# One hybrid encoder step on one core: a held-back last product, an output norm in place, and a later state product

## The chip, the cores and the metric

The kernel runs on one core of one Trainium2 chip. The metric is the device time of one execution in microseconds. The core has five engines that the text speaks of: TensorE (PE, matrix products; PEld is its weight load), VectorE (DVE), ScalarE (ACT), GpSimd (POOL) and SyncE (SP), which here issues every transfer.

## The reference

One layer of a streaming encoder is applied to two kinds of tokens that share all weights: 2048 prompt tokens with zero starting states, and 8 samples of 16 tokens with given states. All data are float32.

```
h = rms_norm(x);  p = h @ w_in
x = x + concat(GDN(p_gdn), RWKV7(p_rwkv)) @ w_out
up = rms_norm(x) @ w_up
gate = causal_dwconv(up[:, :2816])            # width 3, history from state
x = x + (silu(gate) * up[:, 2816:]) @ w_down  # w_down is 2816 x 1024
y = rms_norm(x) * norm_final
# GDN, per chunk:   S = g S + K^T V_new       # one state per sample and head
```

The outputs are y for both kinds of tokens and the new states, among them the gated delta state (GDN) of each sample: 8 samples, 4 heads, 128 x 128.

## The kernel before

Tokens lie along the free dimension, channels along the 128 partitions. The 2176 tokens are cut into five groups of 384, 512, 384, 384 and 512 columns; the fifth holds 384 prompt columns and the 128 sample columns. Each group has an input phase (norm, w_in, convolutions, results to DRAM) and an output phase (w_out, residual, norm, feed-forward network, final norm). The phases run in the order in0, in1, in2, out0, in3, out1, in4, out2, out3, out4. Beside them run two recurrences, GDN and RWKV, block by block of 128 tokens; their small products fill in between the large ones.

**Products.** A float32 product is made of three reduced-precision products: each operand is split into a high part (`whi`, `xh`, `ah`) and a low part (`wlo`, `xl`, `al`), and hi·hi, hi·lo and lo·hi are summed in PSUM (`mm3`). Weights arrive through SP in tiles `w` of up to 512 columns, ACT casts them to `whi` (L439), and DVE or POOL subtracts to get `wlo` (L443). There are four buffers each of `w`, `whi` and `wlo`, and four PSUM banks for the large products.

**The feed-forward part.** `up(i)` makes the gate product `psga` and the value product `psup` for one of 22 feature tiles. Then DVE multiplies `y` by `psup` (L1229), ACT casts the activation to `ah` (L1231), and POOL subtracts to get `al` (L1233). `down` multiplies a part of the activations (parts of 4, 4, 4, 4, 3 and 3 feature tiles) with w_down into eight output tiles `psd`, and DVE adds each to the residual `res[m]` (L1241). For all parts but the last, `down` is called after the first `up` of the next part, so that the newest activation has a whole `up` to become ready. The last part (feature tiles 19, 20, 21) follows its own `up(21)` directly.

**The end of a group.** During the last `down`, ACT squares each `res[m]` and DVE sums the squares into `acc`. The task `finish` starts 3000 ns of the planner's clock later: a product with ones (`psn`), two ACT activations that make the inverse root, then eight times a DVE multiply from `res[k]` into a tile `grs` (L1264) and a store to `y` (L1265, for the last group also L1267). `grs` has two buffers; `res` has eight.

**The order of the work.** A generator-driven planner (`drive`, `spawn`, `step`) writes PE's order by hand: it counts a clock of matmul time, and every `yield n` of a task says that its next products should stand at least n ns of that clock later. The order on the other engines and in SP's queue is set by the tile framework's scheduler, which simulates the program. Every engine executes its own queue in order.

**The sample's states.** In the fifth group's last GDN block, `gdn_block(..., samp=True)`, eight half-head updates are made: DVE masks `w` into `gwm` (L988), the task yields 1500 ns, SP loads the old state `gS`, POOL scales it, PE multiplies `pSs <- gwm, gkt` (128 x 512, plain float32), DVE subtracts it from the state (L995), and SP stores it. The tiles `gwm` and `gS` share the eight buffers of the tag `g2`.

The functions that the change touches and what calls them:

Of the kernel before, what the change touches and what calls it, by code (L numbers as in the profile page):

```python
# [17 lines left out]
MUL, ADD, SUB = ALU.mult, ALU.add, ALU.subtract  # L18
# [183 lines left out]
def bc(a, n):  # L202

    return a.unsqueeze(len(a.shape)).to_broadcast(list(a.shape) + [n])


class Build:
# [236 lines left out]
            out.append((hi, lo))  # L444
        return out

    def mm3(self, ps, w, xs):

        last = len(xs) - 1
        for k, (xh, xl) in enumerate(xs):  # L450
            hi, lo = w[k // 4]
            c = slice(128 * (k % 4), 128 * (k % 4) + 128)
            self.mm(ps, lhsT=hi[:, c], rhs=xh, start=k == 0, stop=False)
            self.mm(ps, lhsT=hi[:, c], rhs=xl, start=False, stop=False)
            self.mm(ps, lhsT=lo[:, c], rhs=xh, start=False, stop=k == last)
            if k % 2 or k == last:
                yield
# [401 lines left out]
    def gdn_block(self, g, i, samp=False):  # L859
        nc, rp = self.nc, self.rp  # L860
# [53 lines left out]
        for p in range(2):  # L914
            ps = self.psr("pKK").rearrange("p (h a t) -> p h a t", h=2, a=2)
# [9 lines left out]
        if samp:  # L925
# [10 lines left out]
            for h in range(4):  # L936
                ps = self.psr("pKS")[:, 0:256].rearrange("p (a t) -> p a t", a=2)
# [23 lines left out]
        w = self.g2("gw", False)  # L961
        nc.scalar.copy(w, pw)
        w = w.rearrange(H4, h=4)
# [19 lines left out]
        if samp:  # L983
            for h in range(4):
                for hf in range(2):
                    c = slice(4 * hf, 4 * hf + 4)
                    wm = self.g2("gwm")
                    nc.vector.tensor_tensor(wm, w[:, h, :].unsqueeze(1).to_broadcast([128, 4, 128]), bc(self.c(C_SEG, 8)[:, c], 128), MUL)  # L988
                    yield 1500
                    S0 = self.g2("gS0")  # L990
                    nc.sync.dma_start(S0, self.I["st_gdn"][h][:, c, :])
                    nc.gpsimd.tensor_tensor(S0, S0, bc(eg[:, h, 64 * hf + 15:64 * hf + 64:16], 128), MUL)
                    ps = self.psr("pSs")
                    self.mm(ps, lhsT=kt[:, h, :], rhs=wm.rearrange("p r t -> p (r t)"), start=True, stop=True)
                    nc.vector.tensor_tensor(S0, S0, ps.rearrange("p (r t) -> p r t", r=4), SUB)  # L995
                    nc.sync.dma_start(self.O["o_gdn_s"][h][:, c, :], S0)
        else:
            pS = self.psr("pS").rearrange(H4, h=4)
            for h in range(4):
                self.mm(pS[:, h, :], lhsT=kt[:, h, :], rhs=w[:, h, :], start=True, stop=True)  # L1000
            for h in range(4):
                nc.vector.scalar_tensor_tensor(SN[:, h, :], SN[:, h, :], eg[:, h, 127:128], pS[:, h, :], op0=MUL, op1=ADD)
# [179 lines left out]
    def phase_out(self, g):  # L1182
        nc, q = self.nc, self.q
        while g.done < 2 or any(t[2] is not None for t in g.tails):
            yield 500
        xs = []
        for k in range(KT):
            xs.append(self.x(g, F32))
            nc.sync.dma_start(xs[k], g.og[k])
        xs = [self.split_x(g, x) for x in xs]  # L1190
        yield LX
        res = []
        for m in range(8):
            w = self.split_w(self.I["w_out"][m])
            ps = self.psb(g, "pso")
            yield from self.mm3(ps, w, xs)
            res.append(self.t(g, "res", 8))
            self.load_tok(g, res[m], self.I["x"][m])
            nc.vector.tensor_tensor(res[m], res[m], ps, ADD)
            if m == 0:  # L1200
                rs = self.acc(g)
            self.sumsq(g, rs, res[m], m == 0)
        hs = [self.split_x(g, res[k], q("nf")[:, k:k + 1]) for k in range(KT)]
        norm = self.spawn(self.late_rms(g, rs, 3000))
        yield LX

        def gate(i, ps):
            y = self.t(g, "xin", NXI)
            self.conv(g, ps, rs, [self.fw[:, 3 * i + n:3 * i + n + 1] for n in range(3)], self.hf[:, i, :], self.sf[:, i], y)
            th = self.t(g, "gth")  # L1210
            nc.scalar.activation(th, y, AF.Tanh)
            nc.vector.scalar_tensor_tensor(y, th, 1.0, y, op0=ADD, op1=MUL)
            nc.gpsimd.tensor_tensor(y, y, rs, MUL)
            return y

        def up(i):
            pair, y = [], None
            for n, name in enumerate(("psga", "psup")):
                w = self.split_w(self.I["w_up"][2 * i + n])
                ps = self.psb(g, name)  # L1220
                yield from self.mm3(ps, w, hs)
                pair.append(ps)
                if n == 0 and norm[2] is None:
                    y = gate(i, ps)
            if y is None:
                yield from self.until(norm)
                y = gate(i, pair[0])
            ps = pair[1]
            nc.vector.tensor_tensor(y, y, ps, MUL)  # L1229
            hi = self.a(g, "ah", F32R)  # L1230
            nc.scalar.copy(hi, y)  # L1231
            lo = self.a(g, "al", F32R)
            nc.gpsimd.tensor_tensor(lo, y, hi.bitcast(F32), SUB)  # L1233
            return hi, lo

        def down(a, b, acts, acc=None):
            for m in range(8):
                w = self.split_w(self.I["w_down"][m][:, 128 * a:128 * b], b - a)
                ps = self.psb(g, "psd")
                yield from self.mm3(ps, w, acts)  # L1240
                nc.vector.tensor_tensor(res[m], res[m], ps, ADD)  # L1241
                if acc is not None:
                    self.sumsq(g, acc, res[m], m == 0)

        acts = {}
        for pi, (a, b) in enumerate(PARTS):
            for i in range(a, b):
                acts[i] = yield from up(i)
                if i == a and pi:
                    pa, pb_ = PARTS[pi - 1]  # L1250
                    yield from down(pa, pb_, [acts.pop(n) for n in range(pa, pb_)])
        pa, pb_ = PARTS[-1]
        acc = self.a(g, "acc")
        yield from down(pa, pb_, [acts.pop(n) for n in range(pa, pb_)], acc)
        self.spawn(self.finish(g, res, acc))

    def finish(self, g, res, rs):

        nc, q = self.nc, self.q
        yield 3000  # L1260
        self.rms(g, rs)
        for k in range(KT):
            y = self.t(g, "grs")
            nc.vector.scalar_tensor_tensor(y, res[k], q("no")[:, k:k + 1], rs, op0=MUL, op1=MUL)  # L1264
            nc.sync.dma_start(self.O["y"][k][:, g.t0:g.t0 + g.P], y[:, 0:g.P])  # L1265
            if g.S:
                nc.sync.dma_start(self.O["y"][k][:, self.tp:self.tp + 128], y[:, g.P:g.n])  # L1267
# [64 lines left out]
```

## Time and profile before

| | |
|---|---|
| median of 3 runs | 3533.35 us (3531.5 to 3534.01) |
| the profiled execution's own time | 3535.21 us |
| its span (first to last instruction) | 3533.4 us |
| PE busy | 3355.5 us (95%), 21661 matmuls |
| DVE / POOL / ACT busy | 2371.1 / 1843.7 / 1512.1 us |
| mean granted TensorE clock | 0.978 |

The kernel is bound by PE nearly everywhere, so its idle time and the stretches at a lower clock are what a change of order can win or lose. In the views below, a row of the timeline gives start and duration in us, engine, line, operation and tiles, and in brackets how long the engine sat idle before it and which instruction ended that. Rows of a line and operation that follow each other closely are merged, with their count.

### The profile page before, as it was taken

Reading aid. Unit: us, or ns where it says so; the run is one execution under the profiler, and the core shown is the slowest. Engines: PE = TensorE matmul, PEld = TensorE weight load, DVE = VectorE, ACT = ScalarE, POOL = GpSimd, SP = SyncE. Lnnn points to the kernel's source line nnn. Section 1 sums busy time; section 2 is a strip of 40 time slices with the busy share of each in tenths; the row PEclk is TensorE's granted clock in tenths of the full one; section 3 lists DMA queues with packets and bytes.
Section 4 is the critical chain, followed back from the end, with each engine's and each line's share of the span. In section 5 each row is a group of like instructions: output and inputs, shape, how many; then the busy total and the mean of one; then the engine's idle time right before and its main releaser. Section 6 shows DMA issues by size and latency. Waiting matters only on the chain. (4 is left out here: it accounts for less than half of the span.)

```text
span 3533.4 us, 60005 instructions
## 1 busy us (share of the span) xinstructions
PE 3355.5 (95%) x21661; PEld 2888.1 (82%) x21661; DVE 2371.1 (67%) x4277; ACT 1512.1 (43%) x2698; POOL 1843.7 (52%) x2335
## 2 busy tenths in 40 slices
PE   8979989999999989999999999899999999999997
PEld 7857778889999878778877667699988899988886
DVE  6777777787666776766565777676657665665444
ACT  5554444444333454443333545443333444453333
POOL 4546556556666545556444445466656355534442
PEclk9989999999999999999999999999999999999999
DMA  5544444453333444533233334533334533443332
GB/s 170 170 127 135 144 151 126 131 174 113 115 114 105 123 145 148 173 93 91 90 93 90 121 120 144 186 116 113 114 119 153 164 120 126 138 143 96 96 94 82
DMA packets 346265, 447.58 MB, mean 127 GB/s; under 512 B 30168, under 2 KB 194336, under 8 KB 345968
## 3 DMA queue, kind: packets, MB, share of 16 engines
q1 hardware_dynamic: 345968, 443.75, 40.5%
q8 instruction: 170, 2.79, 0.3%
q14 instruction: 127, 1.04, 0.1%
HBM read 372.60 MB, written 71.03 MB: 126 GB/s over the span
## 5 line engine op out<-in xcount | busy, mean ns | idle before, releaser
L439 ACT CAST whi<-w 128x512 fp32r<-128x512 f32 (+1 forms) x1070 | 651.4, 610 | 1101.9 <-PE psd L362 282.8
L443 POOL TENSOR_TENSOR wlo<-w,whi 128x512 fp32r<-128x512 f32 (+1 forms) x535 | 705.0, 1318 | 721.9 <-ACT whi L439 695.1
L362 PE MATMUL psi<-x,whi 128*128 128x384 f32 (+1 forms) x2480 | 730.9, 376 | 34.5 <-ACT x L515 16.1
L362 PEld LDWEIGHTS psi<-x,whi 128*128 128x128 f32 x2480 | 454.1, 194 | 96.1 <-issue 21.6
L362 PE MATMUL psga<-x,whi 128*128 128x384 f32 (+1 forms) x1760 | 502.4, 366 | 0.0
L362 PE MATMUL psup<-x,whi 128*128 128x384 f32 (+1 forms) x1760 | 497.1, 363 | 0.0
L443 DVE TENSOR_TENSOR wlo<-w,whi 128x512 fp32r<-128x512 f32 (+1 forms) x535 | 428.2, 800 | 79.5 <-ACT whi L439 78.9
L362 PE MATMUL psi<-x,wlo 128*128 128x384 f32 (+1 forms) x1240 | 453.7, 366 | 4.3 <-POOL wlo L443 4.1
L362 PEld LDWEIGHTS psga<-x,whi 128*128 128x128 f32 x1760 | 318.5, 190 | 28.8 <-issue 3.6
L362 PEld LDWEIGHTS psup<-x,whi 128*128 128x128 f32 x1760 | 315.6, 188 | 26.6 <-issue 1.8
L362 PE MATMUL psd<-ah,whi 128*128 128x384 f32 (+1 forms) x880 | 328.1, 373 | 5.8 <-ACT ah L1231 5.8
L362 PE MATMUL psd<-al,whi 128*128 128x384 f32 (+1 forms) x880 | 318.8, 362 | 5.0 <-POOL al L1233 5.0
L362 PE MATMUL psd<-ah,wlo 128*128 128x384 f32 (+1 forms) x880 | 318.5, 362 | 0.0
L362 PE MATMUL psga<-x,wlo 128*128 128x384 f32 (+1 forms) x880 | 316.3, 359 | 0.0
L362 PE MATMUL psup<-x,wlo 128*128 128x384 f32 (+1 forms) x880 | 314.5, 357 | 0.0
L1241 DVE TENSOR_TENSOR res<-res,psd 128x384 f32<-128x384 f32 (+1 forms) x240 | 145.3, 606 | 201.3 <-PE psd L362 200.2
L362 PEld LDWEIGHTS psi<-x,wlo 128*128 128x128 f32 x1240 | 240.0, 194 | 28.0 <-POOL wlo L443 7.1
L1233 POOL TENSOR_TENSOR al<-xin,ah 128x384 fp32r<-128x384 f32 (+1 forms) x110 | 125.9, 1145 | 143.8 <-ACT ah L1231 103.1
L839 DVE TENSOR_TENSOR TUr<-TUr,pX 128x256 f16<-128x256 f16 x396 | 149.1, 413 | 73.4 <-PE pX L362 72.1
L527 DVE TENSOR_TENSOR P<-psga,rsx 128x384 f32<-128x384 f32 (+1 forms) x110 | 64.3, 585 | 192.9 <-PE psga L362 186.9
L362 PE MATMUL pso<-x,whi 128*128 128x384 f32 (+1 forms) x640 | 185.5, 370 | 2.1 <-DVE x L513 0.9
L362 PEld LDWEIGHTS psd<-ah,whi 128*128 128x128 f32 x880 | 166.6, 189 | 22.0 <-ACT ah L1231 7.2
(342 smaller groups left out, 6759.6 us busy)
## 6 DMA issues: line engine op xcount, KB each, us to landing
w<-in_w_up SPq DMA_DIRECT2D x440, 256.0 KB, 2.7
w<-in_w_in SPq DMA_DIRECT2D x310, 256.0 KB, 2.7
w<-in_w_down SPq DMA_DIRECT2D x160, 256.0 KB, 2.7
rX<-rx SPq DMA_DIRECT2D x68, 320.0 KB, 4.4
w<-in_w_out SPq DMA_DIRECT2D x80, 256.0 KB, 3.0
w<-in_w_down SPq DMA_DIRECT2D x80, 192.0 KB, 2.4
rx<-res SPq DMA_DIRECT2D x48, 192.0 KB, 3.0
gd<-res SPq DMA_DIRECT2D x48, 192.0 KB, 2.8
```

Source lines behind the costliest of these rows:

```text
L362: self.nc.tensor.matmul(out, lhsT=lhsT, rhs=rhs, start=start, stop=stop)
L439: nc.scalar.copy(hi, w)
L443: eng.tensor_tensor(lo, w, hi.bitcast(F32), SUB)
L527: nc.vector.tensor_tensor(P[:, h:h + g.P], ps[:, 0:g.P], rs[:, 0:g.P], MUL)
L839: nc.vector.tensor_tensor(w, w, pX[:, y].rearrange("p u (n b) -> p u n b", b=b), ADD)
L1233: nc.gpsimd.tensor_tensor(lo, y, hi.bitcast(F32), SUB)
L1241: nc.vector.tensor_tensor(res[m], res[m], ps, ADD)
```

## The change

There are three edits and a helper argument.

1. `mm3` takes `part`, a range of feature tiles. `down` takes `lead`. For the last part of each group `lead` is 3: weights and PSUM banks of the first three output tiles are taken at once, the products of feature tiles 19 and 20 are made for all three, and only then those of feature tile 21, the newest. The additions to the residual and the sums of squares of these three follow together. The other five output tiles are done as before. This is done in all five groups.
2. `finish` writes the normalized result over `res[k]` in place of a `grs` tile.
3. The wait of the sample's GDN state task before each state product is 2500 ns of the planner's clock in place of 1500.

```diff
-    def mm3(self, ps, w, xs):
+    def mm3(self, ps, w, xs, part=None):
 
         last = len(xs) - 1
         for k, (xh, xl) in enumerate(xs):
+            if part and not part[0] <= k < part[1]:
+                continue
             hi, lo = w[k // 4]
...
-                    yield 1500
+                    yield 2500
                     S0 = self.g2("gS0")
...
-        def down(a, b, acts, acc=None):
-            for m in range(8):
-                w = self.split_w(self.I["w_down"][m][:, 128 * a:128 * b], b - a)
-                ps = self.psb(g, "psd")
-                yield from self.mm3(ps, w, acts)
+        def down(a, b, acts, acc=None, lead=0):
+            def add(m, ps):
                 nc.vector.tensor_tensor(res[m], res[m], ps, ADD)
                 if acc is not None:
                     self.sumsq(g, acc, res[m], m == 0)
+            weight = lambda m: self.split_w(self.I["w_down"][m][:, 128 * a:128 * b], b - a)
+            first = [(weight(m), self.psb(g, "psd")) for m in range(lead)]
+            for last in range(2):
+                for w, ps in first:
+                    yield from self.mm3(ps, w, acts, (b - a - 1, b - a) if last else (0, b - a - 1))
+            for m, (w, ps) in enumerate(first):
+                add(m, ps)
+            for m in range(lead, 8):
+                w = weight(m)
+                ps = self.psb(g, "psd")
+                yield from self.mm3(ps, w, acts)
+                add(m, ps)
...
-        yield from down(pa, pb_, [acts.pop(n) for n in range(pa, pb_)], acc)
+        yield from down(pa, pb_, [acts.pop(n) for n in range(pa, pb_)], acc, 3)
...
-            y = self.t(g, "grs")
-            nc.vector.scalar_tensor_tensor(y, res[k], q("no")[:, k:k + 1], rs, op0=MUL, op1=MUL)
+            y = res[k]
+            nc.vector.scalar_tensor_tensor(y, y, q("no")[:, k:k + 1], rs, op0=MUL, op1=MUL)
```

Three places in the program's order follow. The first is PE at the start of the last `down` of the fifth group; the number behind a tile's name tells one tile from another, and the newest activation is `ah_39340` before and `ah_39308` now. Before, the whole first output tile:

```order
L362 MATMUL psd_39351<-ah_39008,whi_39347 128x512
L362 MATMUL psd_39351<-al_39010,whi_39347 128x512
L362 MATMUL psd_39351<-ah_39008,wlo_39349 128x512
L362 MATMUL psd_39351<-ah_39242,whi_39347 128x512
L362 MATMUL psd_39351<-al_39244,whi_39347 128x512
L362 MATMUL psd_39351<-ah_39242,wlo_39349 128x512
L362 MATMUL psd_39351<-ah_39340,whi_39347 128x512
L362 MATMUL psd_39351<-al_39342,whi_39347 128x512
L362 MATMUL psd_39351<-ah_39340,wlo_39349 128x512
```

Now, the end of the third tile's two older activations, and then the newest for the first and second tile:

```order
L362 MATMUL psd_39333<-ah_39210,whi_39329 128x512
L362 MATMUL psd_39333<-al_39212,whi_39329 128x512
L362 MATMUL psd_39333<-ah_39210,wlo_39331 128x512
L362 MATMUL psd_39319<-ah_39308,whi_39315 128x512
L362 MATMUL psd_39319<-al_39310,whi_39315 128x512
L362 MATMUL psd_39319<-ah_39308,wlo_39317 128x512
L362 MATMUL psd_39326<-ah_39308,whi_39322 128x512
L362 MATMUL psd_39326<-al_39310,whi_39322 128x512
```

The first use of the newest activation stood behind 6 products of this `down`, and now stands behind 18. In the first group four small products `pR` of a recurrence stand behind the first 12 of them.

The second place is DVE after the second group's last `down`, where the input phase of the fifth group begins (`rsx` is its sum of squares, `x` its split input). Before:

```order
L1264 SCALAR_TENSOR_TENSOR grs<-res,par,acc 128x512 x2
L484 TENSOR_TENSOR rsx<-rsx,xin 128x512
L443 TENSOR_TENSOR wlo<-w_23786,whi 128x512
L484 TENSOR_TENSOR rsx<-rsx,xin 128x512
L1101 TENSOR_REDUCE rs<-pY 128x4
L1264 SCALAR_TENSOR_TENSOR grs<-res,par,acc 128x512
L1138 TENSOR_TENSOR SR<-SRc,pSr 128x128
L1104 TENSOR_TENSOR ryc<-pY,rs 128x256
L1264 SCALAR_TENSOR_TENSOR grs<-res,par,acc 128x512
```

Now:

```order
L486 TENSOR_TENSOR rsx<-rsx,xin 128x512
L1275 SCALAR_TENSOR_TENSOR res<-res,par,acc 128x512 x8
L486 TENSOR_TENSOR rsx<-rsx,xin 128x512
L443 TENSOR_TENSOR wlo<-w_23770,whi 128x512
L1103 TENSOR_REDUCE rs<-pY 128x4
L1140 TENSOR_TENSOR SR<-SRc,pSr 128x128
L486 TENSOR_TENSOR rsx<-rsx,xin 128x512
```

The eight multiplies stood in groups of one or two among other work, and now stand in one run of eight, ahead of the last two additions to `rsx`. A run of eight stands so after each of the first four groups; after the fifth nothing else is left on DVE.

The third place is PE at the sample's first state product. Before:

```order
L362 MATMUL po<-con,gKS 128x128
L362 MATMUL po<-gw,gAQ 128x128
L362 MATMUL pSs<-gwm,gkt 128x512
L362 MATMUL psga<-x,whi 128x384 x2
L362 MATMUL psga<-x,wlo 128x384
L362 MATMUL psga<-x,whi 128x384 x2
```

Now, from the end of the gate product:

```order
L362 MATMUL psga<-x,whi 128x384 x2
L362 MATMUL psga<-x,wlo 128x384
L362 MATMUL pA<-rX 128x256 x4
L372 MATMUL pT_31016<-con,rX 128x128 x3
L362 MATMUL pSs<-gwm,gkt 128x512
L372 MATMUL ptr<-con,ryc 128x128 x2
```

Between the last `po` and the first `pSs` stood nothing; now stand all 24 products of a `psga` and the recurrence's `pA` and `pT`. Ahead of the third state product stand four `pZ` before, and `pZ`, 12 large products and four `pR` now; ahead of the fourth, 6 large products and four `pR` before, and 12 and four `pR` now.

## Prediction

> **What bounds the kernel now.** I read the page first, then the waits of PE, then the timeline of PE with its feeders at the three places that the change touches, and the granted clock there.
>
> ```profile
> span 3533.4 us, 60005 instructions
> PE 3355.5 (95%) x21661; PEld 2888.1 (82%) x21661; DVE 2371.1 (67%) x4277; ACT 1512.1 (43%) x2698; POOL 1843.7 (52%) x2335
> PE pSs L362 <- DVE gwm L988: 7.3, 4, 4.9
> PE psd L362 <- ACT ah L1231: 5.8, 4, 2.0
> PE psd L362 <- POOL al L1233: 5.0, 5, 1.4
> ```
>
> PE is busy for 95% of the span, so 178 us in all are idle. The three waits (us in total, times, longest) are 18.1 us of them: PE waits for the newest activation's high part `ah`, for its low part `al`, and for the masked tile `gwm`. They lie here:
>
> ```profile
> 1212.63 0.34 PE L362 MATMUL psd<-ah,whi 128*128 128x384 f32 x1
> 1213.52 0.34 PE L362 MATMUL psd<-ah,wlo 128*128 128x384 f32 x1
> 1215.79 0.44 PE L362 MATMUL psd<-ah,whi 128*128 128x384 f32 x1 [1.93 <-ACT ah L1231]
> 1217.63 0.69 PE L362 MATMUL psd<-al,whi 128*128 128x384 f32 x1 [1.40 <-POOL al L1233]
> 1983.59 0.39 PE L362 MATMUL psd<-ah,whi 128*128 128x512 f32 x1
> 1986.17 0.49 PE L362 MATMUL psd<-ah,whi 128*128 128x512 f32 x1 [0.90 <-ACT ah L1231]
> 1987.54 0.50 PE L362 MATMUL psd<-al,whi 128*128 128x512 f32 x1 [0.87 <-POOL al L1233]
> 2732.36 0.44 PE L362 MATMUL psd<-al,whi 128*128 128x384 f32 x1 [0.80 <-POOL al L1233]
> 3085.35 0.33 PE L362 MATMUL psd<-ah,whi 128*128 128x384 f32 x1
> 3088.54 0.44 PE L362 MATMUL psd<-ah,whi 128*128 128x384 f32 x1 [2.00 <-ACT ah L1231]
> 3090.08 0.44 PE L362 MATMUL psd<-al,whi 128*128 128x384 f32 x1 [1.09 <-POOL al L1233]
> 3494.25 0.40 PE L362 MATMUL psd<-ah,whi 128*128 128x512 f32 x1
> 3495.41 0.39 PE L362 MATMUL psd<-ah,wlo 128*128 128x512 f32 x1
> 3496.78 0.51 PE L362 MATMUL psd<-ah,whi 128*128 128x512 f32 x1 [0.98 <-ACT ah L1231]
> 3498.13 0.50 PE L362 MATMUL psd<-al,whi 128*128 128x512 f32 x1 [0.84 <-POOL al L1233]
> ```
>
> In each of the five groups PE starts the last `down`, makes the six products of the older activations, and stands still. Six starts span 0.89 us in the first group (five steps of 0.178 us, 384 columns) and 1.16 us in the fifth (0.232 us, 512 columns). The clock after such waits is the eighth number of these windows (span, busy times and counts, PEclk, DMA share, GB/s):
>
> ```profile
> 1217.60:1220.40 2.80, 2.77 (x9) 2.47 (x10) 0.94 (x2) 1.04 (x2) 1.00 (x1) 0.50 0.13 50
> 1988.50:1991.50 3.00, 3.00 (x9) 1.99 (x7) 2.28 (x4) 1.50 (x4) 1.56 (x1) 0.52 0.06 12
> 2732.40:2736.00 3.60, 3.60 (x33) 3.35 (x33) 3.60 (x8) 1.87 (x4) 2.44 (x3) 1.00 0.23 64
> 3091.00:3094.50 3.50, 3.50 (x13) 3.50 (x12) 3.50 (x7) 2.66 (x6) 1.01 (x1) 0.52 0.29 92
> 2646.80:2650.60 3.80, 3.79 (x9) 2.77 (x10) 1.15 (x2) 0.00 (x0) 0.00 (x0) 0.50 0.13 45
> ```
>
> After the waits of the first, second and fourth group the clock is halved for 2.8, 3.0 and 3.5 us, and for 3.8 us after the state wait; after that of the third it stays full. Half of each slow stretch is lost: 1.4, 1.4, 1.7 and 1.9 us.
>
> **Edit 1, the newest product last.** No work is added. `ah` and `al` hang on the `up` ahead, whose rows don't move, so they come when they came; PE now asks for them 18 products after the start. The low part came when the products `psd<-al` above started.
>
> - First group: 18 products, four `pR` (0.28 us by the row at 1250.60 below) and one product of `ah` end at 1212.63 + 19 x 0.178 + 0.28 = 1216.29; `al` is there at 1217.63. 1.34 us of 3.33 stay: gain 2.0.
> - Second: 18 x 0.232 from 1983.59 is 1987.8, `al` is there at 1987.54. All 1.77 go.
> - Third: only 0.80 us is there, and it goes.
> - Fourth: 19 x 0.178 from 3085.35 is 3088.73, `al` is there at 3090.08: 1.35 us of 3.09 stay, gain 1.7.
> - Fifth: 3494.25 + 18 x 0.232 = 3498.43, `al` is there at 3498.13: 1.8 go.
>
> That is 8.1 us. Of the slow stretches I count the second group's 1.4 us as gone, since no wait is left there, and the other two as staying. Edit 1 gains 9.5 us. Its bounds: nothing, if the next products then wait as much longer, and 12.6 with the other two stretches (3.1) gone. Three of four weight buffers are held until the newest products are done; the fifth tile's weights come free behind 21 products and are wanted behind 36, which are 15 x 0.178 = 2.7 us for a cast (0.61) and a POOL subtraction (1.32), by these rows:
>
> ```profile
> L439 ACT CAST whi<-w 128x512 fp32r<-128x512 f32 (+1 forms) x1070 | 651.4, 610 | 1101.9 <-PE psd L362 282.8
> L443 POOL TENSOR_TENSOR wlo<-w,whi 128x512 fp32r<-128x512 f32 (+1 forms) x535 | 705.0, 1318 | 721.9 <-ACT whi L439 695.1
> ```
>
> **Edit 2, the last norm in place.** At the end of the program DVE waits for the stores that empty `grs`:
>
> ```profile
> 3519.52 1.42 DVE L1264 SCALAR_TENSOR_TENSOR grs<-res,par,acc 128x512 f32<-128x512 f32 x2 [3.88 <-ACT acc L502]
> 3522.53 0.75 DVE L1264 SCALAR_TENSOR_TENSOR grs<-res,par,acc 128x512 f32<-128x512 f32 x1 [1.60 <-DMA out_y<-grs]
> 3520.30 0.34 SPq L1265 DMA_DIRECT2D out_y<-grs  x1
> 3521.22 0.38 SPq L1265 DMA_DIRECT2D out_y<-grs  x1
> 3530.65 0.43 SPq L1267 DMA_DIRECT2D out_y<-grs  x1
> DMA packets 2304, 2.10 MB, mean 110 GB/s; under 512 B 256, under 2 KB 2304, under 8 KB 2304
> ```
>
> Without that wait the eight multiplies take 8 x 0.71 = 5.7 us, and SP's pace decides: two stores per tile every 0.92 us (3520.30 to 3521.22). The last store then starts near 3520.30 + 7 x 0.92 + 0.39 = 3527.1, not at 3530.65: gain 3.5 us. The 2.10 MB would flow in some 7 us, 300 GB/s; if they flow slower, down to 250 GB/s, 8.4 us are needed and 2 us are gained. I take 3.5.
>
> After the first four groups the run of eight meets other work. What goes and what comes there:
>
> ```profile
> 1250.60 0.28 PE L362 MATMUL pR<-TUr,Nhr 128*128 128x64 f16 x4 [1.71 <-DVE TUr L839]
> 1249.60 0.62 DVE L1264 SCALAR_TENSOR_TENSOR grs<-res,par,acc 128x384 f32<-128x384 f32 x1 [2.32 <-DMA out_y<-grs]
> 2029.27 0.97 PE L362 MATMUL pA<-rX 64*128 64x256 f32 x4 [2.26 <-ACT rtok L1050]
> 2020.24 1.02 PE L362 MATMUL psn<-rsx,con 128*128 128x512 f32 x2
> ```
>
> In the first group PE waited 1.71 us behind a DVE queue that stood 2.32 us for a store; that goes, and the 2.26 us in the second may. In the second, six more multiplies (6 x 0.7 = 4.2 us) stand ahead of the last additions to `rsx`, for which PE's `psn` at 2020.24 is queued, with all input products behind it: up to 4.2 us come. 1.71 + 2.26 against 4.2 is nothing: I take 0, with bounds of 4 us gained and 6 us lost (4.2 and a slow stretch of 1.9).
>
> **Edit 3, the state product later.**
>
> ```profile
> 2641.54 0.39 PE L362 MATMUL po<-gw,gAQ 128*128 128x128 f32 x2
> 2646.81 2.05 PE L362 MATMUL pSs<-gwm,gkt 128*128 128x512 f32 x2 [4.88 <-DVE gwm L988]
> 2652.89 1.13 PE L362 MATMUL pA<-rX 64*128 64x256 f32 x8
> ```
>
> Between `po` and the first `pSs` now stand 24 products of 384 columns (24 x 0.178 = 4.3 us) and `pA` with its transposes (some 1.1 us by the row at 2652.89). `po` ended near 2641.8, so `pSs` is reached near 2641.8 + 5.4 = 2647.2, after 2646.81: the 4.88 us go, and with them the slow stretch of 1.9. Gain 6.8 us. The three later waits (7.3 - 4.9 = 2.4 us) I leave in, since `gwm` also waits for buffers; with them it is 9.2. The lower bound is 2, if the gate product's weights or a PSUM bank come late in the place to which it is moved up.
>
> **The sum.** 9.5 + 3.5 + 0 + 6.8 = 19.8 us from the span of 3533.4. The profiled execution took 3535.21, 1.8 more than its span, and the median of the runs, 3533.35, stands at the span. So 3533.35 - 19.8 = 3513.6, rounded 3514.
>
> A rule weighed: the Trainium skill (TensorE: Matmul & The Clock Gate, section What's actually happening) says that the clock is halved after an idle window of about 3.4 us, comes back after a busy one, and that the windows run free. The slow stretches here (2.8 to 3.8 us) agree in length; but the second group's waits, 1.77 us together, were followed by one, which the rule does not give. By that rule the 1.3 us that stay in the first and fourth group halve nothing, and the sum would be 22.9 us, 3510.5; that is inside the second case below.
>
> **The rivals.**
> - *All of it goes* (3508): the two slow stretches (3.1) and the three later state waits (2.4) go too. For it: single waits of 0.80 us (third group) left the clock at 1.00, and the state products now stand wider. Against: 1.3 us are more than 0.80.
> - *The waits pass on* (3523): PE comes earlier to the next products and waits there, since DVE and ACT are no faster; the 9.5 us of edit 1 are lost. For it: after the first group PE already waits for DVE (the 1.71 us above), which edit 1 makes no faster; against: the fifth group has nothing behind it but its norm.
>
> - *The change does not do what it says* (3530): the newest product and `gwm` come late again, each behind what was moved ahead of it, and only the end of the program gains 3.5. Against it stand the margins of 0.2 to 0.4 us (second and fifth group, state), worked out above; they are small.
> - *Slower* (3542): the run of eight holds DVE at each of the first four ends, and PE waits it out in full: 3 x 8 x 0.62 + 5.7 = 20.6 us, and four slow stretches of 1.9 (7.6 us), against 19.8 gained. It decides from 5 us a boundary on. For it: `psn` and `wlo` stand behind the run. Against: only the second group's `psn` follows closely enough.
>
> **How the numbers follow.** Chances: forecast 0.43, all goes 0.24, passes on 0.20, not as said 0.07, slower 0.06. What a measurement of this kernel can tell from no change is about 0.2%, 7 us: 3526.3 to 3540.4. Forecast, all goes and the greater part of passes on lie below: faster 0.85; same 0.10, slower 0.05. The range goes from 3504 (the second case, with the 4 us that edit 2 may gain in the middle) to 3526 (the third case with 3 us of edit 2's losses).
>
> **What would show it.** In the changed profile PE's waits for `ah` and `al` should be near 3 us in total, not 10.8, and lie in the first and fourth group; the wait for `gwm` should be under 3 us; no clock of 0.5 at the second group's end and after `po`; the last eight multiplies without a wait for a store, and some 10.5 us from the first of them to the end, not 13.9. A new wait of `psn` for `rsx` after the second group's end of about 4 us would show the price of the run. The prediction is wrong if PE's waits elsewhere, in the first 20 us behind a group's end above all, grow by over 5 us.

## The result and the profile after

The changed kernel took 3515.5 us (median of four executions, 3511.93 to 3515.74) beside 3533.68 of the kernel before: a ratio of 0.9946, 95% interval 0.9935 to 0.9958. The forecast was 3514 in a range of 3504 to 3526. In the experiments the whole change was timed again, five executions beside 17 of the kernel before: a ratio of 0.9958 (0.9944 to 0.9971), which is 14.8 us. So the time came out as forecast, the gain is 15 to 19 us rather than 19.8, and it is not made up as the sum had it.

Of the changed kernel, the span, PE's row, and its waits (us in total, times, longest):

```profile
span 3513.7 us, 59988 instructions
PE 3343.0 (95%) x21661; PEld 2877.8 (82%) x21661; DVE 2377.6 (68%) x4277; ACT 1509.5 (43%) x2698; POOL 1844.4 (52%) x2335
PE pX L362 <- DVE Rr L823: 14.3, 13, 3.4
PE psn L362 <- DVE rsx L486: 8.4, 5, 4.0
PE psn L362 <- DVE acc L486: 8.2, 5, 3.7
PE psd L362 <- POOL al L1235: 2.3, 2, 1.2
PE pSs L362 <- DVE gwm L990: 2.0, 2, 1.3
```

The same waits of the kernel before, those that the prediction didn't show, and two more that the experiments come to (for `rtok` of a recurrence, and for `P` of the input phase):

```profile
PE pX L362 <- DVE Rr L821: 8.1, 9, 2.5
PE pA L362 <- ACT rtok L1050: 6.0, 3, 2.3
PE psg L372 <- DVE P L527: 5.0, 3, 1.8
PE psn L362 <- DVE rsx L484: 4.4, 4, 1.5
PE psn L362 <- DVE acc L484: 3.2, 3, 2.2
```

The waits that the change aims at fell: `psd` from 10.8 to 2.3 us, `pSs` from 7.3 to 2.0. Three others grew by 6.2, 4.0 and 5.0 us. PE's idle time, span less busy time, went from 3533.4 - 3355.5 = 177.9 us to 3513.7 - 3343.0 = 170.7: 7.2 us of 19.7. The other 12.5 us are busy time: the same 21661 matmuls took less, at a mean granted clock of 0.981 in place of 0.978.

Where the two profiles part, read at PE's products with ones (`psn`), which stand once at each norm. Before (the row of the second `rsx` stands in the prediction):

```profile
1234.35 0.91 PE L362 MATMUL psn<-acc,con 128*128 128x384 f32 x2 [0.33 <-DVE acc L484]
1247.03 0.81 PE L362 MATMUL psn<-rsx,con 128*128 128x384 f32 x2
2009.17 1.13 PE L362 MATMUL psn<-acc,con 128*128 128x512 f32 x2
2752.59 0.91 PE L362 MATMUL psn<-acc,con 128*128 128x384 f32 x2 [0.63 <-DVE acc L484]
3105.86 0.81 PE L362 MATMUL psn<-acc,con 128*128 128x384 f32 x2
3515.69 1.13 PE L362 MATMUL psn<-acc,con 128*128 128x512 f32 x2 [2.23 <-DVE acc L484]
```

After:

```profile
1229.75 0.91 PE L362 MATMUL psn<-acc,con 128*128 128x384 f32 x2 [1.24 <-DVE acc L486]
1246.42 0.81 PE L362 MATMUL psn<-rsx,con 128*128 128x384 f32 x2
2001.24 1.12 PE L362 MATMUL psn<-acc,con 128*128 128x512 f32 x2 [0.56 <-DVE acc L486]
2016.14 1.12 PE L362 MATMUL psn<-rsx,con 128*128 128x512 f32 x2 [4.01 <-DVE rsx L486]
2738.47 0.91 PE L362 MATMUL psn<-acc,con 128*128 128x384 f32 x2 [0.43 <-DVE acc L486]
3089.36 1.65 PE L362 MATMUL psn<-acc,con 128*128 128x384 f32 x2 [3.73 <-DVE acc L486]
3498.40 1.92 PE L362 MATMUL psn<-acc,con 128*128 128x512 f32 x2 [2.23 <-DVE acc L486]
```

The lead is 4.6 us at the first group's `acc`, 0.6 at the `rsx` behind it, 7.9 and 4.1 at the second group's pair, 14.1 and 16.5 at the third's and fourth's `acc`, 17.3 at the fifth's, and 19.7 at the end. After the first and the second group 4 us are given back each time. Both times a run of eight multiplies stands in DVE's queue:

```profile
1235.22 5.33 DVE L1275 SCALAR_TENSOR_TENSOR res<-res,par,acc 128x384 f32<-128x384 f32 x8 [0.75 <-ACT acc L504]
2008.36 5.39 DVE L1275 SCALAR_TENSOR_TENSOR res<-res,par,acc 128x512 f32<-128x512 f32 x8 [0.85 <-ACT acc L504]
3503.01 5.39 DVE L1275 SCALAR_TENSOR_TENSOR res<-res,par,acc 128x512 f32<-128x512 f32 x8 [4.67 <-ACT acc L504]
```

In the first group a recurrence's `Rr` is queued behind the run, and PE waits 3.38 us for it; in the second the last additions to `rsx` are, and PE waits 4.01 us. In the third row, at the end of the program, nothing waits: the eight go through, and 3513.7 - 3503.01 = 10.7 us are left from the first of them to the end, where 13.9 were before.

```profile
1241.41 0.28 PE L362 MATMUL pX<-Rr,TUr 128*128 128x64 f16 x4 [3.38 <-DVE Rr L823]
1215.52 0.45 PE L362 MATMUL psd<-al,whi 128*128 128x384 f32 x1 [1.24 <-POOL al L1235]
3073.28 0.45 PE L362 MATMUL psd<-al,whi 128*128 128x384 f32 x1 [1.08 <-POOL al L1235]
```

The last two rows are all that is left of the wait for the newest activation, in the first and fourth group. The windows (the eighth number is the granted clock) behind the first of these waits, behind the 3.38 us, and behind the fourth group's `psn`:

```profile
1217.50:1221.50 4.00, 4.00 (x27) 3.84 (x27) 4.00 (x10) 3.01 (x7) 1.56 (x3) 1.00 0.60 194
1242.00:1245.50 3.50, 3.50 (x14) 3.50 (x13) 1.78 (x4) 0.62 (x1) 0.39 (x1) 0.56 0.74 235
3089.00:3092.50 3.50, 3.14 (x7) 2.19 (x8) 0.30 (x1) 1.44 (x2) 0.00 (x0) 0.51 0.29 105
```

The short wait left the clock whole; the new long ones halved it.

In the third group the wait of 0.80 us for the newest activation is gone too, but PE, which comes earlier, waits longer for a transfer there, the one that brings a recurrence's state `rS`. Before:

```profile
2739.45 1.12 PE L362 MATMUL pZT<-rX,rS 64*64 64x32 f32 x32 [1.01 <-DMA rS<-in_st_rwkv]
```

After, with the window behind it, at half the clock for 6.8 us:

```profile
2722.39 1.12 PE L362 MATMUL pZT<-rX,rS 64*64 64x32 f32 x32 [1.92 <-DMA rS<-in_st_rwkv]
2723.80:2730.60 6.80, 6.80 (x30) 6.80 (x29) 2.28 (x5) 2.14 (x5) 1.48 (x3) 0.50 0.83 255
```

This repeats: the longest such wait in the third group is 0.54 to 1.04 us in all six profiles without edit 1, and 1.71 to 1.92 in all seven with its three tiles, of the two kernels and of the runs below.

### The profile page after: what moved, and what is told of

Its sections match the earlier page's. It is cut to its first block, busy times and chain, and to the rows that moved or that the text cites. A ratio compares the mean times of both kernels' runs of the same rounds, so it can differ in the third digit from the quotient of the medians.

```text
span 3513.7 us, 59988 instructions
## 1 busy us (share of the span) xinstructions
PE 3343.0 (95%) x21661; PEld 2877.8 (82%) x21661; DVE 2377.6 (68%) x4277; ACT 1509.5 (43%) x2698; POOL 1844.4 (52%) x2335
## 3 DMA queue, kind: packets, MB, share of 16 engines
q14 instruction: 127, 1.04, 0.1%
## 5 line engine op out<-in xcount | busy, mean ns | idle before, releaser
L362 PE MATMUL psi<-x,whi 128*128 128x384 f32 (+1 forms) x2480 | 727.0, 374 | 31.2 <-ACT x L517 14.1
L362 PEld LDWEIGHTS psd<-al,whi 128*128 128x128 f32 x880 | 166.3, 189 | 16.6 <-POOL al L1235 2.9
```

What stands on the lines that cost most here:

```text
L362: self.nc.tensor.matmul(out, lhsT=lhsT, rhs=rhs, start=start, stop=stop)
```

## The experiments

My theory after the two traces: edits 1 and 3 remove what they aim at; part of edit 1's gain passes on, because PE now reaches `psn` before DVE has the sum of squares; edit 2 gains at the end and costs, behind the run of eight, about what the waits for stores cost before. The rivals: the single edits are worth their terms in the sum (9.5, 3.5, 6.8); in place costs several us in the middle; or the profiles' differences are chance, since the slow stretches fall differently in every execution. That last one sets the precision: 29 executions of the kernel before, in the first study, lie between 3521.39 and 3539.62 us, with a standard deviation of 4.1. So each verdict below goes by several executions, 5 to 12 of each kernel. The runs come from three studies, each with executions of the kernel before of its own (29, 17 and 17); kernels of different studies are compared by their ratios. "Later sum" in the table means that `finish` of the first four groups waits 6000 ns in place of 3000. Gains in us are the ratio's distance from 1 times 3530, the mean time of the kernel before over the 46 executions of the first two studies (3530.1).

| kernel | ratio to the kernel before | 95% interval | gain, us |
|---|---|---|---|
| edit 1 alone | 0.9990 | 0.9980 to 0.9999 | 3.5 |
| edit 2 alone | 0.9988 | 0.9978 to 0.9998 | 4.2 |
| edit 3 alone | 0.9983 | 0.9974 to 0.9992 | 6.0 |
| whole change | 0.9958 | 0.9944 to 0.9971 | 14.8 |
| all edits, in place in the last group only | 0.9967 | 0.9955 to 0.9979 | 11.6 |
| in place in the last group, nothing else | 0.9985 | 0.9976 to 0.9994 | 5.3 |
| later sum, nothing else | 0.9993 | 0.9984 to 1.0001 | 2.5 |
| edit 1 and later sum | 0.9952 | 0.9939 to 0.9965 | 16.9 |
| whole change and later sum | 0.9932 | 0.9918 to 0.9946 | 24.0 |
| the same, in place in the last group only | 0.9928 | 0.9913 to 0.9943 | 25.4 |
| whole change and later sum, without edit 1 | 0.9959 | 0.9948 to 0.9971 | 14.5 |
| whole change and later sum, `lead` of 4 | 0.9941 | 0.9929 to 0.9953 | 20.8 |

### The edits alone

Edit 1 alone is the change of `mm3` and `down`, with `grs` and 1500 kept:

```diff
-        yield from down(pa, pb_, [acts.pop(n) for n in range(pa, pb_)], acc)
+        yield from down(pa, pb_, [acts.pop(n) for n in range(pa, pb_)], acc, 3)
```

> Edit 1 alone: the newest activation's products come last over three output tiles; the output norm has its own tiles and the state task waits 1500 ns as before. The forecast's terms: 9.5 us off the kernel before (8.1 idle, 1.4 slow clock). The rival that the waits pass on: under 3 us, because PE meets DVE earlier (the changed kernel's wait of 3.73 us for the sum of squares in the fourth group and those for the norm). If the chance placing of slow-clock stretches (1.7 us each in the profiles) dominates, anything from 4 to 15 us, and the runs of this one kernel would differ among themselves by steps of 1.7 us.

It gave 3.5 us. Three of PE's waits in it:

```profile
PE psg L372 <- DVE P L529: 9.1, 3, 4.7
PE psn L362 <- DVE acc L486: 8.1, 5, 3.8
PE pA L362 <- ACT rtok L1052: 8.1, 3, 4.5
```

The 8.5 us at `psd` are gone, as in the whole change (2.3 are left), but `psn<-acc` grew by 4.9 us (3.2 before), `psg<-P` by 4.1 and `pA<-rtok` by 2.1. The longest of the last two (4.7 and 4.5 us) stand after the first and the second group, behind the multiplies into the two `grs` tiles; the next section shows rows of such waits. PE's idle time in this execution is 3525.9 - 3348.6 = 177.3 us, where it was 177.9: the waits passed on in full, and nearly all that its span is shorter by is busy time (6.9 of 7.5 us).

Why PE waits at `psn`, seen in the fourth group. These windows go from the first product of the last `down` to `psn`, before and with edit 1 (span, then the busy times of PE, PEld and DVE):

```profile
3085.35:3105.86 20.51, 17.42 (x86) 16.37 (x86) 17.76 (x30) 13.71 (x26) 7.14 (x7) 0.92 0.54 174
3076.91:3097.75 20.84, 16.00 (x85) 14.55 (x84) 20.12 (x30) 14.89 (x28) 9.24 (x8) 0.98 0.54 183
```

The stretch did not get shorter: what edit 1 takes away at `psd`, PE now waits at `psn`. DVE has the same 30 instructions to do in both, and is now idle for only 0.72 us, so it sets the pace. Its instructions also take 2.4 us longer. Nearly all of that are the seven additions to `acc` (6.91 us against 4.72): three of them took some 1.6 us, each while POOL made a `wlo`, where those that run beside no POOL instruction took 0.55. The product `psn` stands 12 products behind the end of `down` in both. The first three output tiles are now all finished within the last nine of 27 products, so that their additions come in a bunch; whether the bunch costs something by itself isn't shown.

Edit 2 alone:

```diff
-            y = self.t(g, "grs")
-            nc.vector.scalar_tensor_tensor(y, res[k], q("no")[:, k:k + 1], rs, op0=MUL, op1=MUL)
+            y = res[k]
+            nc.vector.scalar_tensor_tensor(y, y, q("no")[:, k:k + 1], rs, op0=MUL, op1=MUL)
```

> Edit 2 alone: the output norm is written over the residual; the rest as before. The forecast's term: 3.5 us off, all of it at the end of the program, the middle nothing. What the changed kernel's profile suggests instead: 2.4 to 3.2 us gained at the end, and about 4 us lost behind the run of eight multiplies after the first group (a wait of PE of 3.4 us) and behind that of the second (4.0 us for rsx), so 0 to 6 us slower than before.

It gave 4.2 us: not slower, so the loss in the middle that I read out of the changed kernel's profile is not the balance. Its waits show the price (8.4 us for `rsx` against 4.4, 13.3 for `Rr` against 8.1), and in part what paid for it: the hold-ups behind the stores fell, `pA<-rtok` from 6.0 to 3.6 us and `psg<-P` from 5.0 to 3.2, and the end of the program gained about 3 us.

```profile
PE pX L362 <- DVE Rr L821: 13.3, 14, 2.4
PE psn L362 <- DVE rsx L484: 8.4, 5, 4.0
```

Edit 3 alone:

```diff
-                    yield 1500
+                    yield 2500
```

> Edit 3 alone: the sample's state task waits 2500 ns; the rest as before. The forecast's term: 6.8 us off (4.9 idle and a slow stretch of 1.9). If the wait for gwm falls as it did in the changed kernel, from 7.3 to 2.0 us, and two slow stretches of 1.7 us go with it, 8.7 us. If PE's gained time is lost at the next wait for DVE, under 3 us.

It gave 6.0 us, and the wait for `gwm` fell from 7.3 us to 1.4, its longest to 0.7. The forecast's term was 6.8.

```profile
PE pSs L362 <- DVE gwm L988: 1.4, 2, 0.7
```

### What in place costs and brings

All three edits, but the first four groups write their norm to the two `grs` tiles (the multiply below the changed line reads `res[k]` again):

```diff
-            y = res[k]
+            y = res[k] if g is self.groups[-1] else self.t(g, "grs")
```

> All three edits, but only the last group's norm is written in place; the first four groups use the two separate tiles as before, so no run of eight multiplies stands in front of the next input phase. If the run of eight costs what the waits behind it suggest (first group 3.4 us and a slow stretch of 1.7; second group 4.0 us less the 2.3 us that the stores cost there before), this is 4 to 8 us faster than the whole change, 3508 to 3512. If in place is worth nothing or something in the middle (the forecast: 0, bounds 4 gained and 6 lost), it is within 2 us of the whole change or slower.

It gave 11.6 us, not more than the whole change's 14.8: the expectation of 4 to 8 us over it is refuted. The run of eight is gone there, and so are its waits, but these came in their place:

```profile
1245.13 0.62 DVE L1275 SCALAR_TENSOR_TENSOR grs<-res,par,acc 128x384 f32<-128x384 f32 x1 [2.16 <-DMA out_y<-grs]
2013.60 0.75 DVE L1275 SCALAR_TENSOR_TENSOR grs<-res,par,acc 128x512 f32<-128x512 f32 x1 [3.49 <-DMA out_y<-grs]
```

```profile
1250.91 0.32 PE L372 MATMUL psg<-con,P 8*128 8x8 f32 x3 [4.66 <-DVE P L529]
2021.57 2.07 PE L362 MATMUL pA<-rX 64*128 64x256 f32 x6 [4.86 <-ACT rtok L1052]
```

DVE's queue stands 2.16 and 3.49 us for a store that empties a tile. Behind the first PE waits 4.66 us for DVE; behind the second it waits 4.86 us for ACT's `rtok`, and that comes from the same queue: ACT itself stood 4.56 us, up to 2014.72, for `ryc`, which is DVE's instruction right behind that store. So after the first two groups in place swaps one hold-up of DVE for another of the same size, and its net there is nothing that these runs can tell from zero.

The same line on the kernel before, with the other edits undone:

> Only the last group's norm is written in place; everything else as in the kernel before. The forecast's term for the end of the program: 3.5 us. By the changed kernel's profile 3.2 us from the first of the eight multiplies to the end (13.9 to 10.7). Edit 2 in all groups gave 4.2 us: if this gives 3 to 3.5, in place in the other four groups is worth about 1 us or nothing; if it gives 6 or more, the run of eight costs there what this gains.

It gave 5.3 us (interval 2.1 to 8.5), which holds both 3.5 and edit 2's 4.2 in all groups. From the first of the eight multiplies (3507.41) to its span's end (3518.1) are 10.7 us, as in the changed kernel: 3.2 gained at the end.

This run also says how far one profile can be trusted. Up to its last eight multiplies, PE, DVE, ACT and POOL have the same instructions in the same order as in the kernel before, and yet PE is idle for 6.9 us less in the first 3500 us (152.2 against 159.1).

### The whole change again, and the sum of squares later

> The whole change again, with many executions beside the same kernel before as its neighbours. If the three edits add up, it is as much faster as the sum of the three alone: 3.5 (edit 1) + 4.2 (edit 2) + 6.0 (edit 3) = 13.7 us by their ratios to the kernel before, a ratio of 0.9961. If the first comparison holds (0.9946 from four executions each), 19 us, and the edits help each other by some 5 us. Executions of one kernel differ by about 4 us (standard deviation in the study of the single edits), so four of them say less than they seemed to.

It gave 14.8 us; the three alone add up to 13.7. They add up, within what these runs can tell.

If edit 1's gain waits at `psn`, moving `psn` back should free it. In `finish`, ahead of the eight multiplies:

```diff
-        yield 3000
+        yield 3000 if g is self.groups[-1] else 6000
```

> The whole change, and the output norm's task of the first four groups waits 6000 ns of the planner's clock in place of 3000, so that psn and the run of eight stand later (all additions to rsx of the next input phase now stand ahead of the run of eight in the first and second group). If edit 1's gain passed on into psn's waits (for acc 3.2 to 8.2 us in total, for rsx 4.4 to 8.4, by the profiles before and after), 5 to 9 us faster than the whole change. If those waits are hidden or come back at the next product, within 2 us of it.

It gave 24.0 us, 9 more than the whole change. The intervals of the two ratios (0.9918 to 0.9946 and 0.9944 to 0.9971) only touch, but the two were timed in the same study, with means of 3506.5 and 3515.5 us over five executions each and standard deviations of 3.7 and 3.3, so the difference is clear of the noise. The wait for `acc` is back at 3.3 us, of which 2.2 stand at the end of the program, that for `rsx` at 4.4, since all additions to it now stand ahead of the run of eight, and that for `Rr` at 8.7. The last line is one of the waits that took their place:

```profile
PE pX L362 <- DVE Rr L823: 8.7, 11, 2.2
PE psn L362 <- DVE rsx L486: 4.4, 4, 1.4
PE psn L362 <- DVE acc L486: 3.3, 2, 2.2
1245.03 0.28 PE L362 MATMUL pR<-TUr,Nhr 128*128 128x64 f16 x4 [2.91 <-DVE TUr L841]
```

The `TUr` that PE waits for here is DVE's first instruction behind the run of eight, which now stands from 1238.20 to 1244.65. So the run still holds up a recurrence, another one of its products.

The same with in place in the last group only:

> As the last, but only the last group's norm in place, the others in their two tiles. If the run of eight is harmless once it stands behind the additions to rsx, equal to the last within 2 us; if it still holds DVE ahead of a recurrence (the wait of 3.4 us for Rr after the first group), 3 to 5 us faster than it. Against all edits with the last group alone in place (0.9967), by the same passing on: 3.7 to 5 us faster.

It gave 25.4 us, the same within its interval. As the wait of 2.91 us shows, the run of eight isn't harmless in the later place; by the times it costs about as much as the two tiles do. These two are the fastest kernels of the study, and both beat the kernel before and the changed one.

Is the later place of `finish` a gain of its own? Two runs take the pair apart: the changed wait of `finish` (6000) on the kernel before, and the same with edit 1.

> The kernel before with the output norm's task of the first four groups at 6000 ns, nothing else. It waits little for acc (3.2 us in total, of which 2.2 stand at the end of the program and stay), so if the later sum only takes back what edit 1 pushed there, 0 to 2 us. If the later place is a gain of its own (the wait for rsx, the two-tile stores behind), 5 us or more, and edit 1's share of the 9 us between the whole change and its version with the later sum is that much less.

> Edit 1 with the output norm's task of the first four groups at 6000 ns; norm in its two tiles and state task at 1500 ns as in the kernel before. Edit 1 alone gave 3.8 us (mean of 11 executions). If its gain was lost to psn's wait for the sum of squares, 8 to 12 us off the kernel before, the forecast's 9.5 for edit 1; if edit 1 never gained more than that, about 4.

Alone it gave 2.5 us, with an interval that holds zero; with edit 1, 16.9. The difference of 14.4 us (about 9 to 20, by the two intervals) is what edit 1 brings where `finish` stands later; beside edit 1 alone (0.9980 to 0.9999) the interval of 0.9939 to 0.9965 is clear. Of edit 1 with the later sum:

```profile
PE psg L372 <- DVE P L529: 4.1, 2, 2.2
PE psn L362 <- DVE acc L486: 3.3, 2, 2.2
```

Not `psn` alone was freed: against edit 1 alone the wait for `acc` fell by 4.8 us, and the hold-up behind the two tiles, `psg<-P`, by 5.0, since the multiplies moved back with it. PE's idle time goes with the times: 177.9 us before, 177.3 with edit 1 alone, 178.1 with the later sum alone, 164.8 with both, a step of 12 to 13 us, where two executions of one order differed by 6.9.

The third run takes edit 1 out of the fast kernel:

```diff
-        yield from down(pa, pb_, [acts.pop(n) for n in range(pa, pb_)], acc, 3)
+        yield from down(pa, pb_, [acts.pop(n) for n in range(pa, pb_)], acc, 0)
```

> The whole change with the later sum of squares (0.9932), but without edit 1: products of the last down in their old order. If edit 1 is worth the forecast's 9.5 us once psn doesn't wait, 3514 to 3516; if it is worth the 3.8 of the run alone, 3508 to 3510.

It gave 14.5 us, 9.5 less than with edit 1 (about 3 to 16, by the two intervals). So with the later sum edit 1 is worth 14.4 us in the one pair and 9.5 in the other, and 3.5 without it. That it is worth more with the later sum than without is shown by the first pair; the second by itself doesn't exclude 3.5, and its profiles have 164.5 us of idle time without edit 1 and 165.8 with it.

### Four output tiles

```diff
-        yield from down(pa, pb_, [acts.pop(n) for n in range(pa, pb_)], acc, 3)
+        yield from down(pa, pb_, [acts.pop(n) for n in range(pa, pb_)], acc, 4)
```

> The whole change with the later sum of squares, but the newest products come last over four output tiles in place of three: 24 products ahead of them. PE still waits 2.3 us for al in the first and fourth group (1.2 us each); six products of 384 columns more (6 x 0.178 = 1.07 us) take most of it, so 2 us faster than with three, and up to 5 if slow stretches go too. All four weight buffers are then held until the newest products are done: if the fifth tile's weights come late, a new wait of PE for wlo of 1 us or more in each group, and 2 to 6 us slower.

It gave 20.8 us against 24.0 with three: no gain, and the intervals overlap. Both halves of the expectation are in its waits, the second in one group only: `al` fell from 2.3 us to 0.4, and in the fourth group `psd` waits 1.3 us for a low part of the weights, which it didn't before. The trace doesn't put that down to the weight buffers: the cast of that tile was done at 3077.79, and DVE, busy with other work, began its subtraction at 3080.65.

```profile
PE psd L362 <- DVE wlo L443: 1.3, 1, 1.3
PE psd L362 <- POOL al L1235: 0.4, 2, 0.2
```

## Why the prediction was right, and where its sum was not

The time, the direction and the range held. Part of the agreement is luck: the sum was taken from 3533.35, the median of three executions, which lies 3 us above the mean of 46, and the gain by the longer comparison is 14.8 us, not 19.8.

- **Edit 1's products: right.** The waits left at `psd` were forecast as 1.34 and 1.35 us in the first and fourth group and none elsewhere; they measured 1.24 and 1.08, 2.3 in total. The 18 products, and what stands ahead of them, were counted rightly from the order and one row.
- **Edit 1's worth: the step that failed.** The sum put it at 9.5 us and gave the case that the waits pass on 0.20. Alone it gave 3.5, and the profile's idle time fell by 0.6. The forecast counted each wait that goes as a gain, and did not ask whether those that PE meets next keep up: in the fourth group DVE, which the group's own sum of squares needs, had only 2.75 us to spare in 20.51, and 3.7 us of wait came back at `psn`; in the third the 0.80 us came back at the transfer of `rS`; and the waits `psg<-P` and `pA<-rtok`, the longest of which (4.68 and 4.50 us) stand after the first and the second group, grew by 4.1 and 2.1. With `finish` moved back, 14.4 and 9.5 us came out, each with a wide interval that holds the 9.5.
- **The rival and the sign.** So the case "the waits pass on" describes edit 1 better than the forecast's own, though its time of 3523 lies further from the measured one. And the sign that the prediction gave for being wrong, waits elsewhere that grow by over 5 us, came: the two aims and the end of the program took away 8.5 + 5.3 + 3.2 = 17.0 us of idle time, the total fell by 7.2, so near 10 came back.
- **The slow stretches behind edit 1: taken with too little.** I let those of the first and fourth group stay, since 1.3 us of wait stay. After the 1.24 us the clock was 1.00. The stretch of the fourth group is there all the same, behind the new wait of 3.73 us at `psn`, and the third group has one of 6.8 us that it didn't have, behind the longer wait for `rS`.
- **Edit 2's end: right.** 3.5 us forecast, 3.2 measured from the first multiply on, in the changed kernel and in the run that has this alone. In the changed kernel's profile 0.8 of it is lost just ahead: the last `psn` took 1.92 us in place of 1.13.
- **Edit 2's middle: right in its sum, and in one of its parts.** A new wait of up to 4.2 us of the second group's `psn` for `rsx` was forecast: 4.01 us. That the waits behind the stores go in exchange was forecast too, and net nothing. That the first group's run would hold up `Rr` (3.38 us) was not seen; nor that, with the two tiles, PE loses as much there once it comes earlier (4.66 and 4.86 us; in the kernel before 1.71 and 2.26).
- **Edit 3: right.** 6.8 us forecast, 6.0 measured alone; the wait for `gwm` under 3 us forecast, 2.0 measured. What stayed is about the 2.4 us that the forecast left in.
- **Idle time and clock.** The sum has 16.5 us of idle time and 3.3 of slow clock. The two profiles have 7.2 and 12.5. That is one execution of each, and how much of the 12.5 belongs to the change and how much to that execution stays open: by the means, the whole change ran at 0.9812 (five executions) and the kernel before at 0.9786 (17).

**The rule weighed** in the prediction, of the Trainium skill (TensorE: Matmul & The Clock Gate, section What's actually happening), fared better here than my reading of one wait, but not throughout. The windows at 0.51 and 0.56 follow waits of 3.73 and 3.38 us, and the 1.24 us that stayed halved nothing, as it gives; the 1.92 us for `rS` are followed by 6.8 us at 0.50, which it does not give, like the second group's 1.77 us before. The same section of the Trainium skill says that the windows run free of the program, so that the slow part falls differently from one execution to the next. The executions of one kernel agree with that: among 29 of the kernel before, the time and the mean granted clock (0.975 to 0.982) go against each other with a correlation of -0.87.

## What to carry to other kernels

When a wait is taken from an engine, follow that engine to its next meetings with the others, and ask of each how much idle time it has left up to there: here DVE had 2.75 us in 20.51, and the gain was lost at the product that needs its sum. Moving that product and the work behind it back by 3000 ns of the planner's clock was worth some 9 us on the whole change. A missing buffer and a long run in a queue can cost the same, so removing the one and making the other is no gain while somebody waits behind the run. And where executions of one kernel have a standard deviation of 4 us, three of them do not fix a baseline to 0.1%.

## What I had not expected of the hardware

Whether idle time halves the clock is not decided by its length alone. Two places of the kernel before: a stretch with idle time and the window after it, and the stretch ahead of the second group's slow window, which the prediction shows at 1988.50 (span, then PE's busy time first, the clock eighth):

```profile
590.50:594.00 3.50, 0.74 (x8) 0.55 (x6) 2.99 (x6) 0.19 (x1) 1.15 (x1) 1.00 0.87 303
594.00:598.00 4.00, 4.00 (x31) 4.00 (x31) 3.96 (x11) 1.79 (x4) 1.69 (x3) 1.00 0.80 247
1984.50:1988.00 3.50, 1.73 (x10) 0.96 (x9) 3.50 (x6) 3.33 (x6) 1.29 (x1) 1.00 0.76 248
```

PE was idle for 2.76 us of the first stretch, and the clock stayed whole; it was idle for 1.77 us of the third, and the clock was then at 0.52. So a wait of 2 or 3 us costs its length and, at some places, half of a slow stretch as well, which is some 1.7 us for the 3.5 us at 0.51 behind the fourth group's `psn`. Which waits pay that can differ with a shift of a few us: the wait for `rS` is followed by a slow stretch in both profiles of the whole change (1.92 and 1.71 us), but not with edit 1 and the later sum alone (1.73 us, clock 1.00).
